# FFN of an encoder trunk on one core: stores on ScalarE's queue, features in one buffer per pair, `down` as one list of 44 steps

## The chip, the cores and the metric

One Trainium2 chip, one core of it. The metric is the device time of one launch in microseconds (us). The kernel computes the whole trunk; nothing is done on the host.

## The reference

Two layers over x of 1024 tokens by 1024 channels, all float32. Each layer has a mixing part (windowed attention, spatial gating, a convolution) and then the two parts that matter here:

```python
hf = rms_norm(x, norm_ffn_g[i]) @ w_gate_up[i]           # 1024 -> 2 x 2816
x = x + (silu(hf[..., :D_FF]) * hf[..., D_FF:]) @ w_down[i]   # D_FF = 2816 -> 1024
gate = sigmoid(rms_norm(x, ple_norm_g[i]) @ w_ple_gate[i])
x = x + (p[i] @ w_ple_proj[i]) * gate
```

## The kernel before

Channels lie on partitions, tokens along the free dimension, in two halves of 512. A float32 product is made of three matmuls: each operand is split into a high and a low half (ScalarE copies the high half, `copy_h`, L122; VectorE subtracts it for the low one, `sub_l`, L125, or L216 in `load_w`), and `step_mm` (L222) adds high x high, high x low and low x high in one PSUM bank.

Gate-up works on 11 pairs of column blocks, 256 columns of gate and 256 of up each, by a scheme with fewer block products than the plain one. `first(j)` makes the plain product of the first column block of pair j with the first token half. It needs only that half, so five of them run ahead, beside the mixing part's end. After the first half of the contraction it stores the partial sum (`s1`, one for gate and one for up) to DRAM, L1139, because `rest` needs it, and at its end the finished features, L1146. `token_forms` then builds five sums and differences of token blocks (`forms`, 20 tiles of 512 tokens in high and low halves). `rest(j)` does what is left of pair j, for gate (i = 0) and then up (i = 1): it loads `s1` (L1182) and two blocks of weights (`rw`, L1185), GpSimd forms sums of weight blocks (L1218 to L1221, the first into half of `ga`), each of five forms is split (`wform`), and five products of four steps each, 12 matmuls, are added in three banks. VectorE takes them out (L1225, L1227, `out_of` at L1211 and L1214), ScalarE makes Silu of the gate (L1212). Features leave in two stores: L1240 for `gb` (the second column block, all tokens) and L1239 for `ga` (the first block, second token half).

The order is `first` 0 to 4, `token_forms`, `first` 5 to 7, and then `rest(0)`, `first(8)`, `rest(1)`, `first(9)`, `rest(2)`, `first(10)`, `rest(3)` to `rest(10)`. So pairs 0 to 2 have a `first` behind them and the last eight have not.

`down` takes 22 blocks of 128 features for each token half, all eight PSUM banks at once. A step loads 128 rows of `w_down` (`load_w`), loads its features (L1296), splits them (`split`) and runs 24 matmuls. After 22 steps VectorE adds the banks to x (L1311), and `norm_add` makes for each of the eight blocks a scaled high half (ScalarE, L122), a low half (VectorE, L128) and squares. Then the second half begins.

Who issues what: all of these loads and stores are on SyncE's queue. The source is in the order told here, but the tile framework, when the kernel is built, reorders the instructions of each engine by its own planning, and an engine then runs its queue in that order. Buffers come from pools: `up` (`U`) with 38 of 4 KB a partition, which holds `forms` (20), the normed first half (8 and one `st`) and all of `rw`, `ga`, `gb`, `ac`, `tf`; `tp` (`T`) with 6 of 2 KB, which holds `s1`, `u2`, `g`, `sg`; `wp` with 3 each for raw weights and their high and low halves.

Of the kernel before, what the change touches and what calls it, by code (L numbers as in the profile page):

```python
# [8 lines left out]
F32 = mybir.dt.float32  # L9
# [62 lines left out]
def tile_encoder_trunk(ctx: ExitStack, tc: tile.TileContext, x, p, positions, norm_mix_g, w_in,  # L72
# [20 lines left out]
    def U(name, dt=F32):  # L93
        return up.tile([P, 1024], dt, tag="u", name=nm(name))

    def T(name, dt=F32):
        return tp.tile([P, 512], dt, tag="tmp", name=nm(name))

    def BA():
        return ps_a.tile([P, 512], F32, tag="a", name=nm("pa"))  # L100

    def BO():
        return ps_o.tile([P, 512], F32, tag="o", name=nm("po"))

    def BT():
        return ps_t.tile([P, 512], F32, tag="t", name=nm("pt"))
# [93 lines left out]
    xd = dp.tile([NK, P, S], F32, name="xd")  # L200

    act_d = [dp.tile([P, S], F32, name=f"act{i}") for i in range(NF)]
    sum_d = [[dp.tile([P, 512], F32, name=f"sum{i}_{j}") for j in range(2)] for i in range(NP2)]


    def load_w(src, shape, eng=None, heng=None):
# [12 lines left out]
    def rows_of(w, r, n, c, m):  # L219
        return w[r:r + n * P, c:c + m].rearrange("(k q) m -> q k m", q=P)  # L220
# [64 lines left out]
    def norm_end(n, bank=None):  # L285
        norm_stat(n)
        norm_bcast(n, bank)
# [174 lines left out]
    for layer in range(DEPTH):  # L462
# [656 lines left out]
        def first(j):  # L1119

            hl0, bc = nrm[0].hl, nrm[0].bc
            c0 = 2 * j * P
            ws = [load_w(rows_of(w_gate_up[layer], 0, NK, off + c0, P), (NK, P),
                         nc.gpsimd if ahead else None, nc.vector if ahead else None)
                  for off in (0, DFF)]
            a = T("sg")
            for i, (wh, wl) in enumerate(ws):
                bank = BA if ahead else BU
                s1 = T("s1")
                for h in range(2):  # L1130
                    b = bank()
                    for k in range(h * HK, (h + 1) * HK):
                        step_mm(b, (wh[:, k, :], wl[:, k, :]), hl0[k], k % HK == 0,
                                k % HK == HK - 1)
                        if k % 2 == 1:
                            bg.tick()
                    if h == 0:
                        nc.vector.tensor_tensor(out=s1, in0=b, in1=bc, op=ALU.mult)
                        nc.sync.dma_start(out=sum_d[j][i], in_=s1)  # L1139
                    else:  # L1140
                        nc.vector.tensor_tensor(out=b, in0=b, in1=bc, op=ALU.mult)
                        nc.vector.tensor_tensor(out=b if i else a, in0=b, in1=s1, op=ALU.add)  # L1142
                if i == 0:
                    nc.scalar.activation(a, a, AF.Silu)
            nc.vector.tensor_tensor(out=a, in0=b, in1=a, op=ALU.mult)
            nc.sync.dma_start(out=act_d[2 * j][:, HALF[0]], in_=a)  # L1146

        forms = [[None] * HK for _ in range(5)]

# [24 lines left out]
            forms[3][k] = split(b21)  # L1174
            forms[4][k] = split(b22)

        def rest(j):

            ga, gb = U("ga"), U("gb")
            for i, off in enumerate((0, DFF)):  # L1180
                s1 = T("s1")
                nc.sync.dma_start(out=s1, in_=sum_d[j][i])  # L1182
                raw = [U("rw").rearrange("p (k m) -> p k m", k=HK) for _ in range(2)]
                for h in range(2):
                    nc.sync.dma_start(out=raw[h], in_=rows_of(w_gate_up[layer], h * HK * P, HK,  # L1185
                                                              off + 2 * j * P, 2 * P))
                a11, a21, a12, a22 = (raw[h][:, :, c * P:(c + 1) * P] for h in range(2)
                                      for c in range(2))
                s3 = ga[:, 0:512].rearrange("p (k m) -> p k m", k=HK)
                tt = nc.gpsimd.tensor_tensor  # L1190
                pool_w = []

                def wform(src):
                    if not pool_w:
                        h = wp.tile([P, 1024], F32R, tag="wh", name=nm("wh"))
                        l = wp.tile([P, 1024], F32R, tag="wl", name=nm("wl"))
                        pool_w.extend((h[:, q * 512:(q + 1) * 512], l[:, q * 512:(q + 1) * 512])
                                      for q in range(2))
                    h, l = (t.rearrange("p (k m) -> p k m", k=HK) for t in pool_w.pop(0))
                    copy_h(h, src)  # L1200
                    sub_l(l, src, h)
                    return h, l

                def prod(b, w, q, start, stop):
                    for k in range(HK):
                        step_mm(b, (w[0][:, k, :], w[1][:, k, :]), forms[q][k],
                                start and k == 0, stop and k == HK - 1, True)

                def out_of(dst, src, b):
                    if i == 0:  # L1210
                        nc.vector.tensor_tensor(out=dst, in0=b, in1=src, op=ALU.add)  # L1211
                        nc.scalar.activation(dst, dst, AF.Silu)  # L1212
                    else:
                        nc.vector.tensor_tensor(out=b, in0=b, in1=src, op=ALU.add)  # L1214
                        nc.vector.tensor_tensor(out=dst, in0=b, in1=dst, op=ALU.mult)

                bank = BT if i else BA
                tt(out=s3, in0=a21, in1=a22, op=ALU.add)  # L1218
                tt(out=a21, in0=a11, in1=a21, op=ALU.subtract)
                tt(out=a11, in0=s3, in1=a11, op=ALU.subtract)  # L1220
                tt(out=a12, in0=a12, in1=a11, op=ALU.subtract)  # L1221
                bb, bd, bc_ = bank(), bank(), bank()
                prod(bb, wform(a11), 0, True, True)
                u2, g = T("u2"), T("g")
                nc.vector.tensor_tensor(out=u2, in0=bb, in1=s1, op=ALU.add)  # L1225
                prod(bd, wform(a21), 1, True, True)
                nc.vector.tensor_tensor(out=g, in0=bd, in1=u2, op=ALU.add)  # L1227
                prod(bc_, wform(s3), 2, True, True)
                if i == 0:
                    out_of(gb[:, 512:1024], g, bc_)  # L1230
                else:
                    nc.vector.tensor_tensor(out=g, in0=bc_, in1=g, op=ALU.add)
                    nc.vector.tensor_tensor(out=gb[:, 512:1024], in0=g, in1=gb[:, 512:1024],
                                            op=ALU.mult)
                prod(bd, wform(a22), 3, False, True)
                out_of(gb[:, 0:512], u2, bd)
                prod(bc_, wform(a12), 4, False, True)
                out_of(ga[:, 512:1024], u2, bc_)
            nc.sync.dma_start(out=act_d[2 * j][:, HALF[1]], in_=ga[:, 512:1024])  # L1239
            nc.sync.dma_start(out=act_d[2 * j + 1], in_=gb)  # L1240

        xpair = [None, None]
        ahead = True
# [12 lines left out]
        for j in range(AHEAD + 1, AHEAD + 1 + BEHIND):  # L1256
            first(j)
        for j in range(NP2):
            rest(j)
            if AHEAD + 1 + BEHIND + j < NP2:  # L1260
                first(AHEAD + 1 + BEHIND + j)
# [26 lines left out]


        nx = [None, None]  # L1290
        for hf in range(2):
            banks = [BO()] + [BA() for _ in range(3)] + [BT() for _ in range(4)]
            for fi in range(NF):
                wh, wl = load_w(rows_of(w_down[layer], fi * P, 1, 0, D), (1, D))
                t = U("ac")[:, 0:512]
                nc.sync.dma_start(out=t, in_=act_d[fi][:, HALF[hf]])  # L1296
                a = split(t)
                for m in range(NK):
                    cs = slice(m * P, (m + 1) * P)
                    step_mm(banks[m], (wh[:, 0, cs], wl[:, 0, cs]), a, fi == 0, fi == NF - 1)  # L1300
                if fi == 8 and hf == 0:
                    proj_weights()
                if fi == 12:
                    xps = [U("X").rearrange("p (m s) -> p m s", m=2) for _ in range(4)]
                    for mp in range(4):
                        nc.sync.dma_start(out=xps[mp], in_=xd[2 * mp:2 * mp + 2, :, HALF[hf]]
                                          .rearrange("m p s -> p m s"))
            nx[hf] = Norm()
            for m in range(NK):
                xo = X[hf][m] = xps[m // 2][:, m % 2]  # L1310
                nc.vector.tensor_tensor(out=xo, in0=banks[m], in1=xo, op=ALU.add)  # L1311
                if hf and m == 0:
                    norm_end(nx[0], BO)
                norm_add(nx[hf], xo, "ple", layer)


        last = layer == DEPTH - 1
# [82 lines left out]
```

## Time and profile before

| | us |
|---|---|
| median of three runs | 2596.1 |
| lowest and highest | 2582.43, 2602.56 |
| the profiled execution | 2591.07 |
| its span, first to last instruction | 2589.2 |
| TensorE busy in it | 2356.6 (91%) |
| mean granted clock of TensorE | 0.955 |

In the profile PE is TensorE's matmuls, PEld its weight loads, DVE VectorE, ACT ScalarE, POOL GpSimd, SP SyncE; SPq and ACTq are instructions of a queue that only issue or wait. Tiles are named as in the code, target first: `wh<-rw` is the high half of a weight made from `rw`. A bracket behind a row of a timeline is the idle time of that engine before it and what ended it. The granted clock is the share of TensorE's full clock, 1.00 for 2.4 GHz and 0.50 for 1.2.

### The profile page before, as it was taken

To read this page: it belongs to the slowest core of one execution; us is meant where nothing else is said; L and a number is where in the kernel's file an instruction comes from. 1 tells how busy PE (TensorE), PEld (TensorE's weight loads), DVE (VectorE), ACT (ScalarE), POOL (GpSimd) and SP (SyncE) were. 2 spreads that over 40 slices of the span, in tenths; PEclk is the share of its full clock that TensorE was granted. 3 is DMA by queue.
4 is the path that set the end of the run, shared out by engine and by line. 5 is a ranking of instruction groups with operands and counts; after the bars stand their busy time and mean duration, and the time that the engine had idled before them with its cause. 6 is when DMAs were issued, how large, how long until landed. Compare 5 with 4: busy or idle time off the path is not lost. (4 is left out here: it accounts for less than half of the span.)

```text
span 2589.2 us, 30142 instructions
## 1 busy us (share of the span) xinstructions
PE 2356.6 (91%) x11404; PEld 1965.9 (76%) x11404; DVE 1555.8 (60%) x2307; ACT 917.6 (35%) x1610; POOL 736.2 (28%) x529
## 2 busy tenths in 40 slices
PE   7998987969998899899999898888899899998999
PEld 6996765857777778688789876676677777886887
DVE  6995675585665553525469666756766565535252
ACT  4346561232222242424323456513222222424242
POOL 4122424541333300103421232435233343001031
PEclk9998998989999999999999999889899999999999
DMA  6111314434333363533321122344333333635332
GB/s 205 40 46 47 133 48 153 149 106 138 110 112 105 104 231 130 177 122 102 98 74 37 34 95 84 98 150 139 118 122 130 106 106 106 231 109 192 102 94 69
DMA packets 243345, 294.77 MB, mean 114 GB/s; under 512 B 11348, under 2 KB 180912, under 8 KB 243200
## 3 DMA queue, kind: packets, MB, share of 16 engines
q1 hardware_dynamic: 236704, 283.16, 33.3%
q10 hardware_dynamic: 6016, 9.45, 1.1%
q8 instruction: 90, 1.47, 0.2%
q0 software_dynamic: 480, 0.24, 0.1%
q14 instruction: 55, 0.45, 0.1%
HBM read 228.84 MB, written 63.96 MB: 113 GB/s over the span
## 5 line engine op out<-in xcount | busy, mean ns | idle before, releaser
L216 DVE TENSOR_TENSOR wl<-raw,wh 128x1024 fp32r<-128x1024 f32 x172 | 217.7, 1266 | 292.9 <-ACT wh L122 285.5
L224 PE MATMUL pt<-tf,wh 128*128 128x512 f32 x792 | 320.1, 406 | 62.1 <-ACT wh L122 62.1
L122 ACT ACTIVATE wh<-raw 128x1024 fp32r<-128x1024 f32 x172 | 182.1, 1059 | 477.6 <-PE pt L226 345.6
L226 PE MATMUL pt<-tf,wh 128*128 128x512 f32 x792 | 317.8, 401 | 0.0
L228 PE MATMUL pt<-tf,wl 128*128 128x512 f32 x792 | 311.4, 398 | 0.0
L264 POOL TENSOR_TENSOR st<-st,sq 128x512 f32<-128x512 f32 x82 | 121.4, 1481 | 578.6 <-ACT sq L263 576.5
L224 PE MATMUL pa<-hl,wh 128*128 128x512 f32 x564 | 232.9, 414 | 48.0 <-DVE sg L1142 32.5
L226 PE MATMUL pa<-tf,wh 128*128 128x512 f32 x704 | 275.3, 391 | 0.0
L228 PE MATMUL pa<-tf,wl 128*128 128x512 f32 x704 | 275.1, 391 | 0.0
L224 PE MATMUL pa<-tf,wh 128*128 128x512 f32 x704 | 273.9, 391 | 0.0
L224 PEld LDWEIGHTS pt<-tf,wh 128*128 128x128 f32 x792 | 155.2, 196 | 103.4 <-ACT wh L122 71.0
L226 PE MATMUL pa<-hl,wh 128*128 128x512 f32 x564 | 229.2, 406 | 2.9 <-DVE hl L128 2.7
L228 PE MATMUL pa<-hl,wl 128*128 128x512 f32 x564 | 227.2, 403 | 0.0
L1218 POOL TENSOR_TENSOR ga<-rw,rw 128x512 f32<-128x512 f32 x44 | 63.8, 1451 | 514.3 <-DMA rw<-in_w_gate_up_dram 486.6
L125 DVE TENSOR_TENSOR wl<-rw,wh 128x512 fp32r<-128x512 f32 x176 | 186.1, 1071 | 30.1 <-ACT wh L122 28.1
L608 PE MATMUL pa<-wh,hl 128*128 128x256 f32 x640 | 179.7, 286 | 4.8 <-ACT zq L621 3.6
L610 PE MATMUL pa<-wl,hl 128*128 128x256 f32 x640 | 181.0, 285 | 0.0
L611 PE MATMUL pa<-wh,hl 128*128 128x256 f32 x640 | 180.2, 285 | 0.0
L226 PEld LDWEIGHTS pt<-tf,wh 128*128 128x128 f32 x792 | 154.6, 195 | 32.4
L228 PEld LDWEIGHTS pt<-tf,wl 128*128 128x128 f32 x792 | 153.3, 194 | 34.0 <-DVE wl L125 1.3
L224 PEld LDWEIGHTS pa<-hl,wh 128*128 128x128 f32 x564 | 111.7, 198 | 77.5 <-DVE sg L1142 34.2
L122 ACT ACTIVATE wh<-rw 128x512 fp32r<-128x512 f32 x176 | 106.2, 623 | 165.1 <-PE pt L226 66.9
(320 smaller groups left out, 5113.4 us busy)
## 6 DMA issues: line engine op xcount, KB each, us to landing
rw<-in_w_gate_up_dram SPq DMA_DIRECT2D x88, 512.0 KB, 5.9
raw<-in_w_down_dram SPq DMA_DIRECT2D x88, 512.0 KB, 3.6
raw<-in_w_gate_up_dram SPq DMA_DIRECT2D x44, 512.0 KB, 4.2
ac<-act SPq DMA_DIRECT2D x88, 256.0 KB, 4.5
raw<-in_w_ple_gate_dram SPq DMA_DIRECT2D x32, 512.0 KB, 4.2
raw<-in_w_in_dram SPq DMA_DIRECT2D x28, 512.0 KB, 3.8
raw<-in_w_out_dram SPq DMA_DIRECT2D x24, 512.0 KB, 3.9
sum<-s SPq DMA_DIRECT2D x44, 256.0 KB, 2.1
```

The source lines that it names most:

```text
L122: nc.scalar.activation(dst, src, AF.Copy, scale=scale)
L125: nc.vector.tensor_tensor(out=dst, in0=src, in1=f(h), op=ALU.subtract)
L216: (eng or nc.vector).tensor_tensor(out=l, in0=raw, in1=f(h), op=ALU.subtract)
L224: nc.tensor.matmul(b, lhsT=wh, rhs=hl[:, 0:512], start=first, stop=False, skip_group_check=again)
L226: nc.tensor.matmul(b, lhsT=wh, rhs=hl[:, 512:1024], start=False, stop=False, skip_group_check=again)
L228: nc.tensor.matmul(b, lhsT=wl, rhs=hl[:, 0:512], start=False, stop=last, skip_group_check=again)
L264: (eng or nc.gpsimd).tensor_tensor(out=n.s, in0=n.s, in1=sq, op=ALU.add)
L608: nc.tensor.matmul(o, lhsT=x_[:, th], rhs=wh, start=(kc + k == 0), stop=False)
L610: nc.tensor.matmul(o, lhsT=x_[:, th], rhs=wl, start=False, stop=False)
L611: nc.tensor.matmul(o, lhsT=x_[:, tl], rhs=wh, start=False, stop=(kc == 1 and k == 3))
L1218: tt(out=s3, in0=a21, in1=a22, op=ALU.add)
```

## The change

Four things are altered.

- The stores of `first` and `rest` (L1139, L1146, L1239, L1240) are issued on ScalarE's queue. The loads stay on SyncE's.
- The two partial sums of a pair go into one tile `sm` of the pool `up` and leave and come back in one transfer each (512 KB, from two of 256 KB). `s1` is a slice of `sm`, in `first` and in `rest`. `ga` is no tile of its own any more: the features of the first column block take the first half of `sm`, which has been read by then. The first sum of GpSimd has a tile `ws` of the pool `tp`.
- All loads of a pair stand in `load_rest(j)`, called right before `rest(j)`: two weight blocks of gate, `sm`, two of up. Before, the loads of up stood in the middle of `rest`.
- `down` is one list of 44 steps. `down_load` of a step, features ahead of weights, stands two steps ahead of its matmuls, across the change of half too; before, each step loaded for itself, and the second half began behind the first one's end.

```diff
-    sum_d = [[dp.tile([P, 512], F32, name=f"sum{i}_{j}") for j in range(2)] for i in range(NP2)]
+    sum_d = [dp.tile([P, S], F32, name=f"sum{i}") for i in range(NP2)]
...
-            a = T("sg")
+            a, sm = T("sg"), U("sm")
...
-                s1 = T("s1")
+                s1 = sm[:, HALF[i]]
...
-                        nc.sync.dma_start(out=sum_d[j][i], in_=s1)
...
+            nc.scalar.dma_start(out=sum_d[j], in_=sm)
             nc.vector.tensor_tensor(out=a, in0=b, in1=a, op=ALU.mult)
-            nc.sync.dma_start(out=act_d[2 * j][:, HALF[0]], in_=a)
+            nc.scalar.dma_start(out=act_d[2 * j][:, HALF[0]], in_=a)
...
-            ga, gb = U("ga"), U("gb")
-            for i, off in enumerate((0, DFF)):
-                s1 = T("s1")
-                nc.sync.dma_start(out=s1, in_=sum_d[j][i])
+        loaded = []
+
+        def load_rest(j):
+            sm, gb, raws = U("sm"), U("gb"), []
+            for i, off in enumerate((0, DFF)):
                 raw = [U("rw").rearrange("p (k m) -> p k m", k=HK) for _ in range(2)]
                 for h in range(2):
                     nc.sync.dma_start(out=raw[h], in_=rows_of(w_gate_up[layer], h * HK * P, HK,
                                                               off + 2 * j * P, 2 * P))
+                if i == 0:
+                    nc.sync.dma_start(out=sm, in_=sum_d[j])
+                raws.append(raw)
+            loaded.append((sm, gb, raws))
+
+        def rest(j):
+
+            sm, gb, raws = loaded.pop(0)
+            ga = sm[:, 0:512]
+            for i, off in enumerate((0, DFF)):
+                s1, raw = sm[:, HALF[i]], raws[i]
...
-                s3 = ga[:, 0:512].rearrange("p (k m) -> p k m", k=HK)
+                s3 = T("ws").rearrange("p (k m) -> p k m", k=HK)
...
-            nc.sync.dma_start(out=act_d[2 * j][:, HALF[1]], in_=ga[:, 512:1024])
-            nc.sync.dma_start(out=act_d[2 * j + 1], in_=gb)
+            nc.scalar.dma_start(out=act_d[2 * j][:, HALF[1]], in_=ga)
+            nc.scalar.dma_start(out=act_d[2 * j + 1], in_=gb)
...
         for j in range(NP2):
+            load_rest(j)
             rest(j)
...
-        for hf in range(2):
-            banks = [BO()] + [BA() for _ in range(3)] + [BT() for _ in range(4)]
-            for fi in range(NF):
-                wh, wl = load_w(rows_of(w_down[layer], fi * P, 1, 0, D), (1, D))
-                t = U("ac")[:, 0:512]
-                nc.sync.dma_start(out=t, in_=act_d[fi][:, HALF[hf]])
-                a = split(t)
+        steps = [(hf, fi) for hf in range(2) for fi in range(NF)]
+        ready = []
+
+        def down_load(hf, fi):
+            t = U("ac")[:, 0:512]
+            nc.sync.dma_start(out=t, in_=act_d[fi][:, HALF[hf]])
+            w = load_w(rows_of(w_down[layer], fi * P, 1, 0, D), (1, D))
+            ready.append((w, split(t)))
+
+        down_load(*steps[0])
+        down_load(*steps[1])
+        for n, (hf, fi) in enumerate(steps):
+            if n + 2 < len(steps):
+                down_load(*steps[n + 2])
+            if fi == 0:
+                banks = [BO()] + [BA() for _ in range(3)] + [BT() for _ in range(4)]
+            (wh, wl), a = ready.pop(0)
+            for m in range(NK):
+                cs = slice(m * P, (m + 1) * P)
+                step_mm(banks[m], (wh[:, 0, cs], wl[:, 0, cs]), a, fi == 0, fi == NF - 1)
```

## Rows read from the trace of the kernel before

**Rows 1.** The page of the profiled execution, its first part (busy time, share of the span, instructions).

```profile
PE 2356.6 (91%) x11404; PEld 1965.9 (76%) x11404; DVE 1555.8 (60%) x2307; ACT 917.6 (35%) x1610; POOL 736.2 (28%) x529
```

**Rows 2.** The waits of TensorE over the whole run: engine, line and tile that waited, what ended the wait, us in total, times, longest.

```profile
PE pt L224 <- ACT wh L122: 62.1, 22, 4.0
...
PE po L224 <- ACT tf L122: 14.6, 2, 7.3
...
PE po L226 <- DVE tf L125: 5.1, 2, 2.6
```

**Rows 3.** The timeline of TensorE, the first and the last of the 60 matmuls of `rest`, i = 0, of the first pair of layer 0 (start, us).

```profile
555.29 0.39 PE L224 MATMUL pa<-tf,wh 128*128 128x512 f32 x1
...
568.66 0.39 PE L228 MATMUL pa<-tf,wl 128*128 128x512 f32 x1
```

**Rows 4.** Windows of layer 0's gate-up: length, then busy us (and instructions) of PE, PEld, DVE, ACT and POOL, the granted clock, the DMA share and GB/s. The first three run from one pair's L1239 store to the next: one pair with a `first` in it, two without. The last is the time right after the idle time at i = 1 of the first pair.

```profile
592.33:634.67 42.34, 39.86 (x169) 32.53 (x168) 25.50 (x33) 10.19 (x17) 11.24 (x8) 0.96 0.39 124
...
716.38:746.78 30.40, 27.49 (x122) 22.44 (x121) 19.48 (x23) 7.66 (x13) 12.17 (x8) 1.00 0.33 113
...
777.77:810.71 32.94, 29.13 (x122) 23.58 (x121) 19.44 (x23) 7.76 (x13) 12.12 (x8) 0.95 0.31 104
...
573.00:576.00 3.00, 3.00 (x8) 2.32 (x8) 3.00 (x3) 0.05 (x1) 2.84 (x3) 0.50 0.02 5
```

**Rows 5.** The timeline of SyncE's queue, some of the L1239 stores, the last of a pair: of layer 0 those of pairs 0, 3 and 9, of layer 1 the same.

```profile
592.33 0.34 SPq L1239 DMA_DIRECT2D act<-ga  x1
...
716.38 0.32 SPq L1239 DMA_DIRECT2D act<-ga  x1
...
907.77 0.32 SPq L1239 DMA_DIRECT2D act<-ga  x1
...
1866.14 0.34 SPq L1239 DMA_DIRECT2D act<-ga  x1
...
1988.87 0.32 SPq L1239 DMA_DIRECT2D act<-ga  x1
...
2182.56 0.32 SPq L1239 DMA_DIRECT2D act<-ga  x1
```

**Rows 6.** The timeline of SyncE's queue at the end of pair 4 of layer 0, in the queue's order (the load of `s1` between them is left out).

```profile
744.06 0.34 SPq L1240 DMA_DIRECT2D act<-gb  x1
...
746.78 0.32 SPq L1239 DMA_DIRECT2D act<-ga  x1
...
747.67 2.05 SPq L1185 DMA_DIRECT2D rw<-in_w_gate_up_dram  x4
```

**Rows 7.** The timelines of GpSimd, ScalarE and TensorE after it: the first and the third sum for i = 1 of pair 5, the copy of its first form, its first matmul (in brackets: idle time before it and what ended it).

```profile
754.05 1.29 POOL L1218 TENSOR_TENSOR ga<-rw,rw 128x512 f32<-128x512 f32 x1 [18.52 <-DMA rw<-in_w_gate_up_dram]
...
756.76 1.26 POOL L1220 TENSOR_TENSOR rw<-ga,rw 128x512 f32<-128x512 f32 x1
...
758.06 0.63 ACT L122 ACTIVATE wh<-rw 128x512 fp32r<-128x512 f32 x1 [0.71 <-POOL rw L1220]
...
758.74 0.50 PE L224 MATMUL pt<-tf,wh 128*128 128x512 f32 x1 [3.49 <-ACT wh L122]
```

**Rows 8.** The waits of SyncE's queue over the whole run, the two stores at the end of a pair.

```profile
SPq L1240 <- DVE gb L1215: 389.2, 22, 26.9
...
SPq L1239 <- DVE ga L1215: 40.1, 22, 2.4
```

**Rows 9.** The timeline of SyncE's queue where layer 0's gate-up ends: the last weight loads and the loads of `pin`.

```profile
908.66 0.96 SPq L1185 DMA_DIRECT2D rw<-in_w_gate_up_dram  x2
...
909.68 1.05 SPq L1266 DMA_DIRECT2D pin<-in_p_dram  x2
```

**Rows 10.** The timelines of VectorE and TensorE at the end of a `first` in layer 0: the product of its features (L1145), and the first matmul of the pair after it.

```profile
599.91 0.69 DVE L1145 TENSOR_TENSOR sg<-pa,sg 128x512 f32<-128x512 f32 x1
...
597.78 0.39 PE L224 MATMUL pa<-tf,wh 128*128 128x512 f32 x1
```

**Rows 11.** Single lines over the whole run (duration of one in ns, least, median and most): a load issued on ScalarE's queue, a store on SyncE's.

```profile
L1089 ACTq DMA_DIRECT2D X<-xd x16: 366/416/482, 365.4 to 1683.1; - x16
...
L1146 SPq DMA_DIRECT2D act<-sg x22: 319/320/1782, 429.5 to 1956.5; - x22
```

**Rows 12.** The timelines of ScalarE, VectorE and TensorE where layer 0's `down` goes from the first token half to the second. VectorE's are the first and the last of the eight adds that free the banks, and the low halves of features; the last row of TensorE begins the second step of the half.

```profile
1060.54 0.61 ACT L122 ACTIVATE tf<-ac 128x512 fp32r<-128x512 f32 x1
...
1049.19 0.69 DVE L1311 TENSOR_TENSOR X<-po,X 128x512 f32<-128x512 f32 x1 [4.03 <-PE po L228]
...
1057.99 0.68 DVE L1311 TENSOR_TENSOR X<-pt,X 128x512 f32<-128x512 f32 x1
...
1066.57 3.08 DVE L125 TENSOR_TENSOR tf<-ac,tf 128x512 fp32r<-128x512 f32 x5
...
1061.21 0.80 PE L224 MATMUL po<-tf,wh 128*128 128x512 f32 x1 [7.30 <-ACT tf L122]
...
1067.30 0.50 PE L226 MATMUL po<-tf,wh 128*128 128x512 f32 x1 [2.55 <-DVE tf L125]
...
1072.65 0.39 PE L224 MATMUL po<-tf,wh 128*128 128x512 f32 x1
```

**Rows 13.** The lines of `rest` that GpSimd and VectorE run on weights, over the whole run (ns, least, median and most).

```profile
L1219 POOL TENSOR_TENSOR rw<-rw x44: 1263/1444/1751, 540.7 to 2191.4; 128x512 f32<-128x512 f32 x44
...
L125 DVE TENSOR_TENSOR wl<-rw,wh x176: 672/684/1819, 548.5 to 2197.4; 128x512 fp32r<-128x512 f32 x176
```

## What the change will do to the time, predicted blind

> **What bounds the kernel now.** I read the page's first part, then the waits of TensorE, then the FFN by windows, then the queues around one joint. TensorE is busy 91% of the span and ScalarE 35% [rows 1], so a change pays only where TensorE stands idle, and ScalarE has room for more work. The largest wait of TensorE in the whole run is for the high half of a weight in gate-up: 62.1 us in 22 times, once in each of the 11 column pairs of each layer; two more, for the token half of `down`, are 14.6 and 5.1 us, one each per layer [rows 2].
>
> What a pair should cost: the 60 matmuls of `rest`, i = 0, start 13.37 us apart from first to last [rows 3], so 13.37 / 59 = 0.2266 us each, 13.6 us for 60, 27.2 for a pair's 120. `first` has 2 x 8 x 3 = 48, 10.9 us, so a pair with a `first` behind it should take 38.1. The windows show 42.3 us for one with a `first`, 30.4 and 32.9 for two without [rows 4]. The six pairs without one take, store to store, 907.77 - 716.38 = 191.4 us in layer 0 and 2182.56 - 1988.87 = 193.7 in layer 1 [rows 5], against 6 x 27.2 = 163.2: 28.2 and 30.5 too much. The three with one take 716.38 - 592.33 = 124.1 and 1988.87 - 1866.14 = 122.7 against 114.3: 9.8 and 8.4 too much. Part of this is the clock: 1.00 in the 30.4 us pair, 0.95 in the 32.9 us one, and after the idle time ahead of one joint the stretch 573 to 576 ran at 0.50, that is 1.2 instead of 2.4 GHz [rows 4]. So a stall costs itself, 62.1 / 22 = 2.8 us in the mean and 4.0 at most, and often (1 - 0.95) x 32.9 = 1.6 more.
>
> Why the stall: SyncE's queue is in order. In it the stores of pair j-1 (L1240, L1239) stand ahead of the weight loads of pair j, i = 1 (L1185). The store at 746.78 waits for the last product of its pair, and the loads leave only at 747.67 [rows 6]. From there 6.4 us to GpSimd's first sum at 754.05, 4.0 to the third at 758.02, ScalarE's copy at 758.06, and the matmul at 758.74 after 3.49 us idle [rows 7]: 11.1 us from issue to product. Those two stores held SyncE's queue for 389.2 and 40.1 us in all [rows 8].
>
> **The change part by part.** *Order.* The tile framework orders each queue when the kernel is built, not by source order alone: the `pin` loads, which need no result, stand directly behind the last weight load [rows 9], though buffers of `up` had long come free (after the last `first`: 38, less 20 of `forms`, is 18, and a pair holds 6). I read from this that a pool gives out its buffers in the order in which the source first touches them. Then `load_rest(j+1)`, though it stands right before `rest(j+1)`, may leave once `gb` of pair j is first written and, where there is one, `sm` of the `first` between.
>
> *Pairs without a `first` (six joints and the pairs between, per layer).* `gb` is first written (L1211) after three of five products of i = 0: 3 x 2.72 = 8.2 us plus 0.7 of VectorE, 9 us into the pair. With no store ahead of them the loads leave then at the latest. 11.1 us later, at 20 of 27.2, the first form of pair j+1 could be ready: 7 us early for i = 0, 20 for i = 1. The forms now need `ws` from the small pool, and it comes behind `g` (L1227), two products or 5.4 plus 0.7 us into a half; 4.0 of GpSimd and 0.6 of ScalarE make 10.7 against 13.6: 2.9 us of cover. That cover would be gone if GpSimd's sums took 1.7 times as long. So I remove the stall and the slow clock behind it, 28.2 + 30.5 = 58.7, and leave 0.2 us a pair: **-56**. Bounds: 0 (loads still late) to -59.
>
> *Pairs with a `first` (j = 1 to 3, and the start of j = 0).* They lose their i = 1 stall: 9.8 + 8.4, and 3 for each j = 0 as for the others: 24. But loads of the next pair now come behind `sm` of the `first`, and the store of its features goes to ScalarE, where copies of the next pair's weights may stand behind it. That store waits for L1145, which ended at 599.91 + 0.69 = 600.60, 2.8 us after the next half's matmuls began at 597.78 [rows 10]; with 0.42 for the issue [rows 11] and 0.6 for the copy, TensorE would start 3.8 us late at four joints a layer: 30 if the copies stand behind the store at all eight, 0 if at none. The later loads speak for behind; I take three quarters, 23. Net **0**; bounds -24 (at none) to +19 (at all, with 1.6 of slow clock at each).
>
> *The stores.* 44 `sum` stores become 22 and move with 66 `act` stores to ScalarE: 88 x 0.42 = 37 us of its sequencer, against 0.32 on SyncE [rows 11]. It lies in ScalarE's idle time (22.7 to 25.2 us of each pair without `first` [rows 4]); queued behind a store that waits are copies, Silu and their users on VectorE and TensorE: priced above and in the last rival. Cost **0**. The merged 512 KB reload of `sm` replaces two of 256 KB: no bytes more, **0**. VectorE and GpSimd do the same operations.
>
> *`down` as one list.* At the change of half ScalarE copies the high half of step 22's features only at 1060.54, behind eight norm copies, and VectorE their low half from 1066.57. TensorE waits 7.30 us to 1061.21 and 2.55 to 1067.30; the second step begins at 1072.65. VectorE's eight adds, which free the banks, start at 1049.19 and end at 1058.67 [rows 12]. With features of steps 22 and 23 fetched two steps ahead, only the adds hold it: the step ends at 1058.67 + 0.7 = 1059.4, 13.3 us earlier. Step 24's features still come behind the eight copies; I leave 2.8 us for that. 10.5 in each layer: **-21**, bounds 0 to -30. Inside a half nothing waits now, and nothing is gained.
>
> Sum: -56 + 0 - 21 = -77 against the profiled 2591.1: 2514. The median of the runs is 5.0 higher, so **2519**.
>
> **The rivals.** *A: all of it.* The copies stand ahead of the stores and the first pairs gain as well: -59 - 24 - 26 = -109, 2487. For it: the copies of a next pair's i = 0 stand early today. Against: their loads also came a pair early, and now do not.
>
> *B: half.* GpSimd or VectorE becomes the wait in i = 1. GpSimd's sums took 1.26 to 1.75 us and VectorE's low halves 0.67 to 1.82 [rows 13]; with the longest, 3 x 1.75 + 0.6 + 1.8 = 7.7 behind 6.1 is 13.8, past the 13.6, and whatever delays them more is a stall. If of 4.7 us a pair 2.5 stay: -77 + 12 x 2.5 = -47, 2549.
>
> *C: the loads are no earlier.* A queue of its own saves only issue time: 110 stores at 0.32 us, none of it where TensorE waits. Then only `down` gains: about 2575, and with half of that 2586. Against it the queue's order [rows 6] and its 389 us behind one store [rows 8]. The Trainium skill, DMA: Bandwidth & Descriptors, section "Issuing engines are not separate DMA queues", says just this: all transfers share the same 16 engines, and spreading over issuers saves the sequencer's time alone. The rows disagree where an issue waits, for a wait is sequencer time that is not small; by the page the sum would be rival C's, by the rows it is mine.
>
> *D: slower.* The wait moves to ScalarE: at the end of every pair the copy of the next pair's first form stands behind the store of `ga`. From the figures above: 2.8 + 0.42 + 0.6 = 3.8, and 1.6 of slow clock: 5.4 us at 22 joints: +119, against 83 + 21 removed: +15, 2611. It decides from 104 / 5.4, or 20 of 22 joints on. Against it: forms of i = 0 of pair j+1 should be ready 7 us before the pair ends, so the planner has no reason to queue them behind its last store.
>
> **How the numbers follow.** My forecast, 2495 to 2535, has 0.47; A, down to 2465, 0.17; B and mixtures up to 2570, 0.16; C 0.11; D 0.09. The range takes mine, A and B: 2470 to 2570, leaving out 2 in 10. Within 1% (2570 to 2622) is about what a measurement can't tell from no change: C and, in D, nearly half: faster 0.80, same 0.15, slower 0.05.
>
> **What would show it.** Right, if in the pairs after the last `first` SyncE's L1185 loads leave without a store ahead of them and a pair takes 27 to 28 us at clock 1.00; if the row of TensorE waiting for the copied weight falls from 62.1 us below 25 with what is left behind a `first`; if no eight norm copies stand between the last step of one half and the features of the next, and that gap is near 10 us to the step's end. Wrong, if GpSimd still waits for `rw` with TensorE idle (C), if ScalarE's idle rows name DMA issues or VectorE's L1215 ahead of `wh` copies (D), or if the clock is below 1.00 in pairs without a stall.

## The result, and the profile after

The changed kernel takes 2507.9 us (median of four runs, 2507.2 to 2509.7) against 2596.9 for the kernel before on the same chip (four runs, 2582.4 to 2602.6): ratio 0.967, 95% interval 0.963 to 0.971, faster. The prediction, 2519 with a range of 2470 to 2570, holds the time. The profiled execution took 2507.3 us with a span of 2505.5 and a mean granted clock of 0.967; the one before 2591.1, 2589.2 and 0.955. So the span is 83.7 us shorter, where the sum of the prediction said 77.

First the page's first part, as in [rows 1]: engine, busy us, share of the span, instructions.

```profile
PE 2327.1 (93%) x11404; PEld 1950.1 (78%) x11404; DVE 1493.4 (60%) x2307; ACT 915.8 (37%) x1610; POOL 730.1 (29%) x529
```

The same 11404 matmuls are 29.5 us shorter in sum. No matmul was taken out: this is time in which they ran at a lower clock, as in the pairs of [rows 4], where the same 122 took 29.13 us at 0.95 and 27.49 at 1.00. The rest of the 83.7 us is idle time of TensorE that is gone. The waits of TensorE over the whole run say which:

```profile
PE pt L224 <- DVE sm L1138: 36.9, 2, 18.6
PE pa L224 <- ACT wh L122: 23.5, 8, 4.2
...
PE po L226 <- DVE tf L125: 1.6, 2, 0.8
```

The row of 62.1 us in 22 times [rows 2] is gone; eight waits for a copied weight are left, on the banks `pa` (i = 0), where before they were on `pt` (i = 1). In `down` the 14.6 us are gone and 1.6 are left of the 5.1. The first row belongs to the start of gate-up, where the five `first` run ahead; it was 32.5 us for `sg` and 10.4 for `s` in the kernel before, and is 36.9 for `sm` and 10.9 for `sg` now, 5 us more.

The windows of layer 0's gate-up answer to [rows 4]: one pair with a `first`, two without, and a stretch across the change of half in `down`. The columns are those of [rows 4].

```profile
632.62:674.80 42.18, 39.97 (x170) 32.60 (x169) 25.70 (x32) 10.30 (x16) 12.00 (x8) 0.96 0.36 125
712.68:739.88 27.20, 27.20 (x122) 22.52 (x121) 14.81 (x23) 7.56 (x13) 11.01 (x9) 1.00 0.37 126
848.68:875.88 27.20, 27.20 (x122) 22.52 (x121) 14.81 (x23) 7.56 (x13) 9.87 (x8) 1.00 0.19 68
1015.00:1030.00 15.00, 15.00 (x68) 12.43 (x67) 12.00 (x14) 11.83 (x19) 7.37 (x5) 1.00 0.25 87
```

A pair without a `first` takes 27.20 us with TensorE busy all the time at clock 1.00: what its matmuls alone were worked out to take. The pair with a `first` takes 42.18 at 0.96, as before (42.34). In the stretch across the change of half in `down` TensorE does not stop.

Summed by stage, from the same marks before and after (last store of a pair; first of the eight adds of a half), and for both layers:

| stage | before, us | after, us | both layers |
|---|---|---|---|
| pair 0 to pair 3 (three with a `first`) | 124.1, 122.7 | 123.1, 124.7 | +1.0 |
| pair 3 to pair 9 (six without) | 191.4, 193.7 | 163.2, 163.2 | -58.7 |
| half to half of `down` | 133.2, 133.2 | 120.8, 120.8 | -24.7 |
| all else | | | -1.3 |

The table is the prediction's own list of terms: -56, 0 and -21. What it can't show is whether they came about as the prediction said. The signs that the prediction named for being right came too: pairs of 27.20 us at clock 1.00 with no store ahead of their loads, 23.5 us of waits (below 25) left behind a `first`, no norm copies ahead of the features of steps 22 and 23 (ScalarE had copied both by 970 us). But they don't tell which of the altered parts brought it about. Three readings cast doubt on the prediction's. The first is the queue of SyncE at pair 5 of layer 0, as in [rows 6]:

```profile
741.97 0.92 SPq L1184 DMA_DIRECT2D rw<-in_w_gate_up_dram  x2
...
743.54 26.57 SPq L1184 DMA_DIRECT2D rw<-in_w_gate_up_dram  x4
```

No store stands among the loads, as predicted. They are earlier than forecast: counted through the queue, the two that leave at 741.97, 2.1 us after the last store of pair 4 (739.88), are gate's of pair 7. Those of pair 6 were forecast for 9 us into pair 5 at the latest. But the group of four behind them (up's of pair 7, gate's of pair 8) takes 26.57 us to issue, for it now waits for buffers. Over the run SyncE waits longest there for tiles whose store is still landing:

```profile
SPq L1184 <- DMA act<-sm: 238.3, 10, 24.7
```

It was 389.2 us for one store [rows 8]; the 238.3 of now cost TensorE nothing, for all these pairs take 27.20 us. The length of a wait in this queue doesn't say what it costs. The second reading is ScalarE's queue in the same pair:

```profile
746.56 0.63 ACT L1222 ACTIVATE gb<-gb 128x512 f32<-128x512 f32 x1 [8.43 <-DVE gb L1221]
747.10 1.14 ACT L122 ACTIVATE wh<-rw 128x512 fp32r<-128x512 f32 x2
...
749.45 0.62 ACT L1222 ACTIVATE gb<-gb 128x512 f32<-128x512 f32 x1
751.13 0.63 ACT L122 ACTIVATE wh<-rw 128x512 fp32r<-128x512 f32 x1 [1.06 <-PE pa L226]
752.00 0.63 ACT L1222 ACTIVATE sm<-sm 128x512 f32<-128x512 f32 x1 [0.24 <-DVE sm L1221]
```

The copies of the weights for up (`wh<-rw`) stand between the three Silus of gate (L1222). The third reading is the joint behind the first `first`, on SyncE, GpSimd, ScalarE and TensorE; the prediction expected copies behind the store of the features (L1146) there.

```profile
579.55 6.72 SPq L211 DMA_DIRECT2D raw<-in_w_gate_up_dram  x2
586.38 1.21 SPq L1184 DMA_DIRECT2D rw<-in_w_gate_up_dram  x2
...
594.25 1.29 POOL L1228 TENSOR_TENSOR ws<-rw,rw 128x512 f32<-128x512 f32 x1 [38.61 <-DMA rw<-in_w_gate_up_dram]
...
598.26 0.63 ACT L122 ACTIVATE wh<-rw 128x512 fp32r<-128x512 f32 x1 [0.71 <-POOL rw L1230]
...
602.82 0.33 ACTq L1146 DMA_DIRECT2D act<-sg  x1
...
598.95 0.50 PE L224 MATMUL pa<-tf,wh 128*128 128x512 f32 x1 [2.97 <-ACT wh L122]
```

The copies stand ahead of the store. TensorE waits 2.97 us, but from ScalarE back to GpSimd back to the loads: they left at 586.38, behind the raw loads of `first` (L211), which had waited for a buffer.

### The profile page after: what moved, and what is told of

Same layout as the page of the kernel before. It is cut to its first block, busy times and chain, and to the rows that moved or that the text cites. A ratio compares the mean times of both kernels' runs of the same rounds, so it can differ in the third digit from the quotient of the medians.

```text
span 2505.5 us, 30172 instructions
## 1 busy us (share of the span) xinstructions
PE 2327.1 (93%) x11404; PEld 1950.1 (78%) x11404; DVE 1493.4 (60%) x2307; ACT 915.8 (37%) x1610; POOL 730.1 (29%) x529
## 5 line engine op out<-in xcount | busy, mean ns | idle before, releaser
L226 PE MATMUL pt<-tf,wh 128*128 128x512 f32 x792 | 308.2, 389 | 0.0
L224 PE MATMUL pt<-tf,wh 128*128 128x512 f32 x792 | 306.1, 390 | 0.0
L228 PE MATMUL pt<-tf,wl 128*128 128x512 f32 x792 | 304.6, 389 | 0.0
L224 PE MATMUL pa<-tf,wh 128*128 128x512 f32 x704 | 277.3, 396 | 23.5 <-ACT wh L122 23.5
L226 PE MATMUL pa<-tf,wh 128*128 128x512 f32 x704 | 278.2, 395 | 0.0
L224 PE MATMUL pa<-hl,wh 128*128 128x512 f32 x564 | 228.1, 406 | 16.4 <-DVE sg L1141 10.9
L226 PE MATMUL pa<-hl,wh 128*128 128x512 f32 x564 | 225.6, 400 | 2.9 <-DVE hl L128 2.7
L1228 POOL TENSOR_TENSOR ws<-rw,rw 128x512 f32<-128x512 f32 x44 | 70.1, 1593 | 410.6 <-DMA rw<-in_w_gate_up_dram 214.6
L224 PEld LDWEIGHTS pa<-tf,wh 128*128 128x128 f32 x704 | 134.7, 191 | 55.1 <-ACT wh L122 26.9
L224 PEld LDWEIGHTS pt<-tf,wh 128*128 128x128 f32 x792 | 148.7, 188 | 30.9
L226 PEld LDWEIGHTS pt<-tf,wh 128*128 128x128 f32 x792 | 148.7, 188 | 30.6
L125 DVE TENSOR_TENSOR wl<-rw,wh 128x512 fp32r<-128x512 f32 x176 | 140.8, 804 | 32.5 <-ACT wh L122 32.4
L228 PEld LDWEIGHTS pa<-tf,wl 128*128 128x128 f32 x704 | 134.2, 191 | 28.6
```

The source lines that it names most:

```text
L125: nc.vector.tensor_tensor(out=dst, in0=src, in1=f(h), op=ALU.subtract)
L224: nc.tensor.matmul(b, lhsT=wh, rhs=hl[:, 0:512], start=first, stop=False, skip_group_check=again)
L226: nc.tensor.matmul(b, lhsT=wh, rhs=hl[:, 512:1024], start=False, stop=False, skip_group_check=again)
L228: nc.tensor.matmul(b, lhsT=wl, rhs=hl[:, 0:512], start=False, stop=last, skip_group_check=again)
```

## The experiments

Each kernel was timed in three rounds beside the kernel before. The expectations give the theories by letters: Q, that the stall was the stores in SyncE's queue; O, that it was the order in which the instructions stand on the other engines too, ScalarE's above all; L, that at the joints with a `first` the loads are late; what else they name is told in them. A ratio is to the kernel before.

| run | what it is | us | ratio | 95% interval |
|---|---|---|---|---|
| e1 | before, stores on ScalarE | 2574.0 | 0.992 | 0.989 to 0.995 |
| e2 | after, stores on SyncE | 2511.0 | 0.967 | 0.965 to 0.970 |
| e3 | before, `down` as one list | 2571.1 | 0.991 | 0.988 to 0.993 |
| e4 | after, `load_rest` ahead of the `first` | 2478.5 | 0.954 | 0.952 to 0.957 |
| e5 | e4, `load_rest(0)` as in after | 2480.4 | 0.956 | 0.954 to 0.958 |
| e6 | e5, stores on SyncE | 2484.2 | 0.957 | 0.955 to 0.959 |
| e7 | before, loads of up beside gate's | 2515.2 | 0.969 | 0.967 to 0.971 |
| e8 | e7 and `down` as one list | 2491.7 | 0.960 | 0.958 to 0.962 |
| e9 | e8, stores on ScalarE | 2490.1 | 0.960 | 0.956 to 0.963 |

### e1: only the stores

```diff
-                        nc.sync.dma_start(out=sum_d[j][i], in_=s1)
+                        nc.scalar.dma_start(out=sum_d[j][i], in_=s1)
...
-            nc.sync.dma_start(out=act_d[2 * j + 1], in_=gb)
+            nc.scalar.dma_start(out=act_d[2 * j + 1], in_=gb)
```

(So for all four stores, L1139, L1146, L1239 and L1240.)

> The kernel before with one part of the change: its stores (L1139, L1146, L1239, L1240) on ScalarE's queue, all else as it was. Theory Q (the stores ahead of the loads on SyncE are the whole cause): the loads leave early, the wait for the copied weight (62.1 us in 22) is gone and the six pairs without a first take 27.2 us: -59 or more, about 2538. Theory O (the order of all queues, which follows from where the loads stand in the source, is the cause): the loads leave early, but in ScalarE's queue the copies for up still stand behind the last Silu of gate, as they do before; from the last matmul of gate 0.7 us of VectorE, 0.6 of Silu and 0.6 to 1.2 of copies make a stall of 2.0 to 2.5 us where it was 3.4, and the gain is 12 x 1 plus some slow clock: -10 to -25, 2572 to 2587.

It gains 20.5 us, a quarter of the whole. All 22 waits stay, a little shorter:

```profile
PE pt L224 <- ACT wh L122: 52.8, 22, 2.5
```

The timelines of one pair of layer 0 say why: SyncE, GpSimd, ScalarE, TensorE.

```profile
734.87 2.04 SPq L1185 DMA_DIRECT2D rw<-in_w_gate_up_dram  x4
...
743.25 1.29 POOL L1218 TENSOR_TENSOR ga<-rw,rw 128x512 f32<-128x512 f32 x1 [18.85 <-DVE wl L125]
...
755.75 0.63 ACT L1212 ACTIVATE ga<-ga 128x512 f32<-128x512 f32 x1 [2.09 <-DVE ga L1211]
756.28 1.13 ACT L122 ACTIVATE wh<-rw 128x512 fp32r<-128x512 f32 x2
...
757.47 0.80 PE L224 MATMUL pt<-tf,wh 128*128 128x512 f32 x1 [2.48 <-ACT wh L122]
```

The loads now leave at 734.87, 12.5 us ahead of the pair's last store (747.41 on ScalarE's queue): the move does what the prediction said of it. GpSimd begins its sums for up at 743.25, 14.2 us ahead of the product that needs them; before, these were 4.7 [rows 7]. And still TensorE waits 2.48 us, because in ScalarE's queue the copies for up stand behind all three Silus of gate, and the last of these needs the last product of gate. The kernel before has the same order, here its third Silu of pair 5 and the first copy for up:

```profile
756.01 0.63 ACT L1212 ACTIVATE ga<-ga 128x512 f32<-128x512 f32 x1 [2.09 <-DVE ga L1211]
756.72 0.63 ACT L122 ACTIVATE wh<-rw 128x512 fp32r<-128x512 f32 x1
```

So the loads were not the last thing that came late: the order on ScalarE was behind them, and it stayed as it was. Beside its own length a stall can cost clock, but it doesn't always. In the windows below the clock falls to 0.55 right behind this idle time, while behind the same 2.48 us a pair earlier (the matmul at 727.45) it stayed at 1.00.

```profile
727.00:730.00 3.00, 2.55 (x11) 2.10 (x12) 3.00 (x5) 1.96 (x4) 0.00 (x0) 1.00 0.02 5
...
754.00:757.00 3.00, 0.98 (x5) 0.48 (x3) 0.76 (x2) 1.25 (x3) 0.43 (x1) 1.00 0.00 0
757.00:760.00 3.00, 2.53 (x6) 2.07 (x7) 3.00 (x5) 1.98 (x4) 0.00 (x0) 0.55 0.00 0
```

The six pairs of layer 0 go on in this way, in turn about 30.0 us at clock 1.00 and 31.5 at 0.95. Together they take 184.5 us, in layer 1 184.4: for both layers 16.2 less than before, where the whole change took off 58.7.

### e2: the whole change with its stores back on SyncE

```diff
-            nc.scalar.dma_start(out=act_d[2 * j][:, HALF[1]], in_=ga)
-            nc.scalar.dma_start(out=act_d[2 * j + 1], in_=gb)
+            nc.sync.dma_start(out=act_d[2 * j][:, HALF[1]], in_=ga)
+            nc.sync.dma_start(out=act_d[2 * j + 1], in_=gb)
```

(And the same for the two stores of `first`.)

> The changed kernel with its stores (sum and act) back on SyncE's queue; the loads in load_rest, sm, ws and the list of down stay. Theory Q: the loads wait behind the stores again and the six pairs take 30 to 33 us as before; only down gains: about 2570. Theory O: in SyncE's queue the loads of a pair now stand behind the store of the pair two before it, so they still come early enough, the six pairs take 27.2 us each, and the time is that of the change, 2503 to 2515.

It takes 2511.0, with an interval that takes in the ratio of the whole change, and its six pairs take 27.20 us each. SyncE's queue waits for a store almost as long as before (389.2 [rows 8]):

```profile
SPq L1250 <- DVE gb L1225: 336.0, 22, 21.7
```

and in it the loads stand behind the stores again:

```profile
740.03 0.34 SPq L1249 DMA_DIRECT2D act<-sm  x1
740.42 1.03 SPq L1184 DMA_DIRECT2D rw<-in_w_gate_up_dram  x2
```

TensorE does not wait for them in these pairs: in the built program's queue the loads behind the stores of pair j are gate and up of pair j+2, so they are a pair early even behind the store. GpSimd does (13.10 us ahead of its sum at 746.00), at no cost in time. With the loads placed as the change places them, the move of the stores is worth nothing that these runs can tell.

### e3: only `down` as one list

The diff is that of `down` in the change.

> The kernel before with the list of 44 steps in down alone. Between the last add of one half and that of the next the change took 12.35 us off in each layer; if the parts don't meet, that is all that moves here: -25, about 2572, with the six pairs of gate-up at 30 to 34 us as before. Rival: the features of the second half come early only because SyncE's queue has lost the stores; then nothing or little, about 2592.

It gains 23.3 us. Half to half takes 120.8 us in both layers, as in the changed kernel, and of TensorE's waits in `down` only this one is left; gate-up's row is no smaller than before (62.1):

```profile
PE pt L224 <- ACT wh L122: 65.9, 22, 5.4
...
PE po L226 <- DVE tf L125: 1.6, 2, 0.8
```

So `down` adds its part by itself. e1 and e3 together are 44 of the 89 us. The rest must be in what neither has: the place of the loads and the tiles.

### e7: only the place of the loads for up

Stores, tiles and `down` are those of the kernel before. The loads of up move from the middle of `rest` to its head.

```diff
+            got = []
             for i, off in enumerate((0, DFF)):
                 s1 = T("s1")
                 nc.sync.dma_start(out=s1, in_=sum_d[j][i])
...
+                got.append((s1, raw))
+            for i in range(2):
+                s1, raw = got[i]
```

> The kernel before with one part of load_rest: the loads for up (s1 and two blocks of weights) stand at the head of rest, beside those for gate, and no longer in its middle. Stores stay on SyncE, s1 and ga and the two transfers of the sums stay, down stays. Theory O: this alone makes the copies for up stand ahead of the Silu of gate in ScalarE's queue; the six pairs take 27.2 to 27.5 us, -59, about 2535. Theory Q: nothing has left SyncE's queue, the pairs take 30 to 33 us as before, 2585 to 2600.

This alone gains 79.8 us, more than the 59 of the six pairs. All 22 waits for a copied weight in gate-up are gone, and the stores are still in SyncE's queue ahead of the loads: here the last store of pair 4, the loads behind it, and the last store of pair 5.

```profile
731.90 0.32 SPq L1243 DMA_DIRECT2D act<-ga  x1
732.27 2.14 SPq L1186 DMA_DIRECT2D rw<-in_w_gate_up_dram  x4
...
759.10 0.32 SPq L1243 DMA_DIRECT2D act<-ga  x1
```

A pair takes 759.10 - 731.90 = 27.20 us. The same four loads stand at the same place as in [rows 6], 0.4 us behind the last store; but they are other loads. In the built program's queue the four behind the stores of pair j were up of j+1 and gate of j+2; now they are both of j+2. ScalarE's queue changed with it:

```profile
734.78 0.63 ACT L1216 ACTIVATE gb<-gb 128x512 f32<-128x512 f32 x1 [2.47 <-DVE gb L1215]
737.06 0.63 ACT L122 ACTIVATE wh<-ga 128x512 fp32r<-128x512 f32 x1 [1.65 <-PE pa L226]
...
738.12 0.62 ACT L1216 ACTIVATE gb<-gb 128x512 f32<-128x512 f32 x1
741.84 0.63 ACT L122 ACTIVATE wh<-rw 128x512 fp32r<-128x512 f32 x1 [3.10 <-PE pa L226]
742.71 0.63 ACT L1216 ACTIVATE ga<-ga 128x512 f32<-128x512 f32 x1 [0.24 <-DVE ga L1215]
```

Copies stand between the Silus, as in the changed kernel. With its loads early, the planner puts up's work among gate's on GpSimd, ScalarE and TensorE alike. The three pairs with a `first` gain too: the stores at 589.47, 627.55 and 665.63 are 38.08 us apart, what the prediction gave for such a pair without a stall. In exchange `down` begins with a wait of 4.3 us in each layer.

### e4, e5, e6: the loads at the joints with a `first`

In e4 `load_rest` stands ahead of the `first` that comes between, and `load_rest(0)` ahead of `first` 5 to 7. e5 puts `load_rest(0)` back behind them. e6 is e5 with the stores on SyncE (the edit of e2).

```diff
+        load_rest(0)
         for j in range(AHEAD + 1, AHEAD + 1 + BEHIND):
             first(j)
         for j in range(NP2):
-            load_rest(j)
             rest(j)
+            if j + 1 < NP2:
+                load_rest(j + 1)
             if AHEAD + 1 + BEHIND + j < NP2:
                 first(AHEAD + 1 + BEHIND + j)
```

> The changed kernel with load_rest(j+1) called ahead of the first that follows rest(j), and load_rest(0) ahead of first 5 to 7. Theory L (behind a first the loads of the next pair are late, because the sm of that first is touched ahead of them in the source, and so they stand late in SyncE's queue): the eight waits of 23.5 us for the copied weight at i = 0 shrink to a few us, and with the slow clock behind them 20 to 35 us go: 2473 to 2488. Theory S of the prediction (copies stand behind the store of the first's features on ScalarE): the stall stays, 2500 to 2512.

e4 takes 2478.5 us, 29 less than the changed kernel. The eight waits of 23.5 us for a copied weight are two of 2.5 us; the largest row of TensorE's waits is another:

```profile
PE pt L224 <- DVE sm L1138: 49.6, 2, 24.9
...
PE pa L224 <- ACT wh L122: 2.5, 2, 1.9
```

GpSimd's sums for the pair behind the first `first` are early, where the changed kernel had it waiting for `rw` until 594.25:

```profile
585.52 1.29 POOL L1228 TENSOR_TENSOR ws<-rw,rw 128x512 f32<-128x512 f32 x1 [7.93 <-DVE gb L1243]
```

and the stores of ScalarE at the ends of pairs 0 and 1, at 593.90 and 632.01, are 38.11 us apart. So the loads were late there, and no store held anything up. The row of `sm` rose by 12.7 us (36.9 before): the wait at the start of gate-up is longer with the loads of pair 0 ahead of `first` 5 to 7.

> As e4, but with load_rest(0) behind first 5 to 7 again, so that only the loads of pairs 1 to 10 stand ahead of the first between. In e4 the wait of TensorE for VectorE's evacuation (sm, L1138) in the stage of token_forms rose from 18.6 to 24.9 us in each layer. Theory: that is the price of having pair 0's loads (and what they release on GpSimd, ScalarE and VectorE) in that stage; it goes back to 18.6, two waits of 3 to 4 us at pair 0 come back, and the time is 3 to 10 us below e4: 2468 to 2476. Rival: the stage only changed its order by chance, and e5 is within 2 us of e4.

e5 takes that wait back and gives up some of it elsewhere:

```profile
PE pt L224 <- DVE sm L1138: 37.0, 2, 18.6
...
PE pa L224 <- ACT wh L122: 7.9, 2, 3.9
```

12.6 us less at the start and 5.4 more for copied weights, yet the time is 2480.4, not below e4's. That expectation was missed; within these intervals the two are the same. In the two traces e5 is 4.8 us ahead at the end of layer 0's `down` (its second half's first add at 1127.21 against 1132.03) and 0.4 at the end of pair 0 of layer 1 (1811.18 against 1811.58); what took the rest in between stays open.

> e5 with its stores on SyncE's queue. If the order of loads to products is all that counts, stores ahead of them cost nothing as long as the loads are for a pair or two later: within 5 us of e5. If the queue matters once the loads of pairs 1 to 3 are tight, these wait behind the stores of the pair before: 10 to 25 us above e5.

e6 takes 2484.2 against 2480.4. The intervals of the ratios overlap, but the fastest of its four runs (2483.5) is slower than the slowest of e5's (2481.8), and the longest wait for a copied weight is 8.3 us in it against 3.9, so these 4 us are likely real. They are far from the 56 that the prediction hung on this queue.

### e8, e9: the small edits together

e8 is e7 with `down` as one list, and e9 is e8 with the stores on ScalarE.

> e7 with the list of 44 steps in down; stores on SyncE, s1, ga and the order of pairs and firsts as in the kernel before. If the two parts add up: e7's -80 and e3's -25 (by spans), 2485 to 2492. In e7 TensorE waits 4.3 us where down begins, its feature load at 890.62 standing behind the store at 889.07 in SyncE's queue; the list has the features ahead of the weights, but not ahead of that store, so this wait stays.

2491.7 us: the gains of e7 and e3 add up (79.8 + 23.3 = 103.1; measured 104.9). These two edits alone beat the changed kernel by 16 us, without the tiles `sm` and `ws` and the merged transfers; e9 tells why. The wait at the start of `down` stays, 4.3 us a layer.

> e8 with its stores on ScalarE's queue, as in the change. Theory: the store in SyncE's queue costs only where down begins; there 4.3 us in each layer go, and nothing else moves: 3 to 10 us below e8. Rival: stores on ScalarE hold copies in the pairs with a first, and e9 is no faster than e8 or slower.

2490.1: the move of the stores is worth nothing here either, and the 3 to 10 us expected of it were missed. Where they were sought, at the start of `down`, the wait is still 4.37 us. The rows are of SyncE and TensorE.

```profile
888.42 7.43 SPq L211 DMA_DIRECT2D raw<-in_w_down_dram  x2
895.94 0.41 SPq L1300 DMA_DIRECT2D ac<-act  x1
...
900.59 0.59 PE L224 MATMUL po<-tf,wh 128*128 128x512 f32 x1 [4.37 <-ACT tf L122]
```

The first features are loaded behind two loads of raw weights, which took 7.43 us to issue. It is again a load's place among loads, not a store.

e9 shows one thing more. From the changed kernel it differs in the tiles, with the partial sums in two transfers each; the place of the loads in the source is the same, right before `rest`, behind the `first`. Yet its loads of pair 1 leave 35.5 us ahead of the last store of pair 0 (594.78). In the changed kernel they left 3.3 us ahead of it (586.38 and 589.63).

```profile
559.29 7.39 SPq L1186 DMA_DIRECT2D rw<-in_w_gate_up_dram  x4
```

From pair 0 to pair 3 it takes 115.2 us in each layer, against 123.1 and 124.7 in the changed kernel: 17.3 less in all, about the whole 17.8 us between the two kernels. So the tiles, or the merged transfers that come with them, made the loads late behind a `first`, as the prediction read it from the pools, and either the old tiles (e9) or the loads ahead of the `first` (e4) cure that.

## Why the prediction was right in time and wrong in cause

**Pairs without a `first`: -56, measured -58.7.** The size was read from the gap between 27.2 us of matmuls and the windows, with the clock's share in it, and that held to 3 us (the 0.2 us a pair left over were not needed). The step that failed is "Why the stall: SyncE's queue is in order. In it the stores of pair j-1 stand ahead of the weight loads of pair j". Both are true, and the loads did come late. But the stores alone, taken out of the queue, left 52.8 of the 62.1 us of waits and took 16.2 us off these pairs (e1), and put back under the change they brought none of it back here (e2: 27.20 us a pair). What sets it is which loads stand behind the store: those of the half that is next, or of a pair later (e7). And the source's place of the loads sets ScalarE's order too; the prediction looked for a copy behind a store there, not behind a Silu.

**The 389 us.** Offered against rival C, they were no evidence. A queue that is early can wait 336 us in all and cost nothing (e2). What counts is whether an engine sits idle behind the waiting instruction.

**Rival C and the page beside it.** The Trainium skill, DMA: Bandwidth & Descriptors, section "Issuing engines are not separate DMA queues", gives no more than the sequencer's time for such a move. Where the loads stand early, the runs agree: the move is worth 3.1 us (e2 against the changed kernel), 3.7 (e6 against e5) and 1.6 (e8 against e9), and only the 3.7 is clear of the spread of the runs. Where they stand late, the move was worth 20.5 us (e1), since there the sequencer's time includes a wait that counts. As a forecast C was wrong in its time (2575), since it took the change to be the move of the stores; of that move it said more rightly what it is worth than the forecast did.

**Pairs with a `first`: 0, measured +1.0.** Right in size, wrong in cause. That the loads come late behind `sm` held (e9 with the old tiles has them early), though they stood behind raw loads of the `first` that waited for a buffer. The step "copies of the next pair's weights may stand behind" the store failed: in the trace they stand ahead of it. The late loads themselves used up what there was to gain: with them early, e4 takes 29 us less and e7 gains at these joints too. The prediction took the late loads as a reason for the order on ScalarE, and gave them no price of their own; it comes to 17.3 us (e9), where the 23 had been set down for the copies.

**Stores on ScalarE: 0.** An issue took 0.326 us there, not the 0.42 of a load [rows 11], and nothing waited for it; rival D did not happen. The row is of all 22 stores of L1250 (least, median, most in ns).

```profile
L1250 ACTq DMA_DIRECT2D act<-gb x22: 326/326/327, 584.8 to 2137.9; - x22
```

**`down`: -21, measured -24.7 from half to half, the same alone (e3, whose time fell by 23.3).** The mechanism was right: no norm copies stand ahead of the features of steps 22 and 23, and step 24's still come behind all eight. ScalarE makes their high half at 1029.36, right behind the last of its norm work, and VectorE their low half at 1035.50. The 2.8 us left for that wait were 0.8.

```profile
1028.84 0.61 ACT L263 ACTIVATE sq<-X 128x512 f32<-128x512 f32 x1
1029.36 0.62 ACT L122 ACTIVATE tf<-ac 128x512 fp32r<-128x512 f32 x1
...
1035.50 1.28 DVE L125 TENSOR_TENSOR tf<-ac,tf 128x512 fp32r<-128x512 f32 x2
...
1036.23 0.50 PE L226 MATMUL po<-tf,wh 128*128 128x512 f32 x1 [0.82 <-DVE tf L125]
```

**Rival A** would have been near for another order of the loads: e4 takes 2478.5, and A gave 2487.

**What stays open.** No run altered ScalarE's order by itself: the change and e7 move the loads and that order together, and e1 shows only what is left when the loads alone are early. Which of `sm`, `ws` and the merged transfers makes the loads late behind a `first` was not tried apart; that it is `sm`, in the pool of the loads, is the reading of the pools. Why in e1 only every second of equal stalls is followed by a slow clock was not followed.

## What to carry to other kernels

A wait in an in-order queue is a cost only if an engine starves behind it: ask what stands behind the waiting instruction and when that is needed, before the length of the wait is taken as a gain. Where a planner orders the engines, moving a load in the source changes the order of everything that hangs on it; read the order on each engine between load and matmul, and try each part of a change alone. Here the smallest edit, loads of the second half at the head of the first, gave 80 of the 89 us. The loads ahead of the work between gave 29 more, over half of which the new tiles had cost: new tiles can hold up loads whose place nobody moved.

## What the runs showed of the hardware

In e1 TensorE stood idle for 2.48 us up to 727.45 and again up to 757.47, busy without a gap in between. Behind the first stall the granted clock stayed at 1.00; behind the second it was 0.55 over 3 us, near 1.2 instead of 2.4 GHz. The pairs with these stalls were 30.0 and 31.5 us long (717.40 to 747.41 to 778.95 by their last stores) against 27.20 without, so equal stalls cost 2.8 and 4.3 us. Issuing a store took 0.326 us on ScalarE and 0.32 to 0.34 on SyncE, so neither is the cheaper place for it.
